# Output projection of the second half: all eight input tiles in one PSUM tile

## The chip, the cores and the metric

The kernel runs on one core of one Trainium2 chip. The metric is the device time of one execution in microseconds; the median of three executions is given. The engines are called as in the profile: PE (TensorE, matrix products), PEld (its weight loads), DVE (VectorE), ACT (ScalarE), POOL (GpSimd) and SP (SyncE, which issues most of the transfers). Each engine works through its own queue of instructions in order, and waits where an operand or a buffer isn't ready.

## The reference

One layer of a decoder, for 512 prompt tokens and 8 x 4 sample tokens (544 columns). A feed-forward block (FFN1), a mixing block and a second feed-forward block (FFN2), with a layer norm behind each:

```
x   = layer_norm(ALPHA * x + 0.5 * swiglu(x, ffn1), ln1)
proj = x @ w_in
y_rwkv = RWKV-7 recurrence over 8 heads of 64 (group norm, gate)   # 512 features
y_conv = c_b * conv3(c_c * c_h)                                    # 512 features
mix = concat(y_rwkv, y_conv) @ w_out                               # 1024 x 1024
x   = layer_norm(ALPHA * x + mix, ln2)
x   = layer_norm(ALPHA * x + 0.5 * swiglu(x, ffn2), ln3)
```

The change is in `mix` and in the sum that the second layer norm takes its mean from.

## The kernel before, in words

Features lie on the 128 partitions, tokens on the columns. So 1024 features are 8 tiles (`KD`), and the 544 columns are two halves, `HALF` = 0 to 256 and 256 to 544 (288 columns). Every product is done as three passes in a split format: weights and inputs are each split in a high part and a low part. `xhl` holds the input of the current product, split so. `mm3` (L146) issues for each input tile the matmuls high x high (L150), high x low (L151) and low x high (L152), and accumulates them in one PSUM tile. PSUM tiles named `mm` come from a pool of three (`big`), those named `sm` from a pool of five.

A weight tile is loaded by `wload` (L113): SP issues a 512 KB transfer into a tile `raw`; ACT writes the high part into a tile `hl` (`wsplit`, L134); DVE writes the low part (L135). A raw tile is free when both are done, an hl tile when its last matmul is done. Around the change there are two raw tiles and four hl tiles (three of the pool `wp` and one of `w4`). When FFN2 is opened (`f2.open`), three raw and three hl tiles are added, in memory that earlier stages have left, and the loads that use them may run ahead.

The 1024 input features of the output projection are eight tiles. Tiles 4 to 7 are the convolution part, tiles 0 and 1 the first two pairs of heads, tiles 2 and 3 the last two pairs, which the recurrence finishes last. The weights are packed to fit: `wo_c` has tiles 4 to 7 for two output tiles a load, `wo_0` tiles 0 and 1 for four output tiles, `wo_1` tiles 2 and 3 for four output tiles. `wout(h)` (L1402) does tiles 4 to 7, 0 and 1 of one half: 18 matmuls for each output tile `d`, and a DVE addition into `z` (L1420). `last(h)` (L1423) does tiles 2 and 3: 6 matmuls for each output tile, a second DVE addition into `z` (L1431), and an addition to the running sum over output tiles (`add_sum`, L320 and L322), from which the layer norm takes the mean.

The order of work is made by generators. `bg` is a queue of work that fills gaps; `take` runs its first generator for a given amount, and `weave` runs a generator on the critical chain (`gnorm`, `layer_norm`) and takes fill between its steps. A scheduler then sets the place of every instruction on its engine. Behind the recurrence come `last(0)` and the group norm of the last heads; then the layer norm of the first half, `l2a`, with `wout(1)` as fill; then the pools of the mixing block are closed, FFN2's are opened, `last(1)` runs by itself, and the layer norm of the second half, `l2b`, runs with `f2.first()` as fill (the gate and up products of FFN2's first four row tiles, for the first half). In `layer_norm` the sum (L222 for `l2b`, L227 and L228 for `l2a`) gives the mean, L235 subtracts it, L236 squares, L241 or L243 add the squares, L248 or again L222 sum them, L255 and L258 make the factor, L262 and L268 apply it, and L138 and L139 split the result into `xhl`.

Of the kernel before, what the change touches and what calls it, by code (L numbers as in the profile page):

```python
# [15 lines left out]
OP = mybir.AluOpType  # L16
# [13 lines left out]
HALF = ((0, 256), (256, 544))  # L30
# [31 lines left out]
def body(ctx: ExitStack, tc: tile.TileContext, xT, gu1, wd1, win, wo_c, wo_0, wo_1, gu2, wd2, lora, vec, cst,  # L62
         sst, cstate, s0, y_o, wkvp_o, wkvs_o, shift_o, conv_o):
    nc = tc.nc
    PE, ACT, DVE, POOL = nc.tensor, nc.scalar, nc.vector, nc.gpsimd
# [13 lines left out]
    xhl = keep.tile([P, 2, KD, T], F32R, name="xhl")  # L79
# [10 lines left out]
    def big():  # L90
        return ps.tile([P, 512], F32, name="mm", bufs=3)

    def sm():
        return ps.tile([P, 512], F32, name="sm", bufs=5)
# [15 lines left out]
    def wtiles():  # L110
        return raw_tile(), hl_tile()

    def wload(src, n=1024, parts=1):  # L113
        raw, hl = wtiles()
        m = n // parts
        for i in range(parts):
            dma(raw[:, i * m:i * m + m], src[:, i * m:i * m + m])
            wsplit(hl, raw, i * m, i * m + m)
        return hl

    def issue(prev, f, *args, **kw):
        with tc.issue_after(prev.ins):
            return f(*args, **kw)

    def after(ins, prev):
        info = mybir.DependencyInfo(mybir.DependencyClass.NoSync, mybir.DependencyReason.DATA)
        tc.add_manual_dep(ins.ins, prev.ins.name, info, reason="table order")
# [5 lines left out]
    def wsplit(hl, raw, a, b):  # L133
        ACT.activation(hl[:, 0, a:b], raw[:, a:b], AF.Copy)  # L134
        DVE.tensor_tensor(hl[:, 1, a:b], raw[:, a:b], hl[:, 0, a:b].bitcast(F32), op=OP.subtract)  # L135

    def split(hi, lo, x):
        ACT.activation(hi, x, AF.Copy)  # L138
        DVE.tensor_tensor(lo, x, hi.bitcast(F32), op=OP.subtract)  # L139

    def block(hl, j, i):
        if isinstance(hl, tuple):
            hl, i = hl[i // 4], i % 4
        return hl[:, j, i * P:(i + 1) * P]

    def mm3(out, hl, src, ks, c0, c1, off=0, start=True, stop=True):  # L146
        n = len(ks)
        for i, k in enumerate(ks):
            wh, wl = (block(hl, j, off + i) for j in range(2))
            PE.matmul(out, wh, src[:, 0, k, c0:c1], start=(start and i == 0), stop=False)  # L150
            PE.matmul(out, wh, src[:, 1, k, c0:c1], start=False, stop=False)  # L151
            seen["fill"] = PE.matmul(out, wl, src[:, 0, k, c0:c1], start=False, stop=(stop and i == n - 1))  # L152
            if i % 2 and not (stop and i == n - 1):
                yield 6 * ((c1 - c0) / 2.4 + 3)

    bg = deque()
# [22 lines left out]
    def take(need):  # L179
        while need > 0 and bg:  # L180
            g = bg[0]
            try:
                need -= next(g)
            except StopIteration:
                bg.popleft()

    def until(done):
        while not done():
            take(1)
# [10 lines left out]
    def weave(key, crit, *fill):  # L200
        bg.extend(fill)
        for need in crit:
            take(need * FILL[key])

    def drain(*fill):
        bg.extend(fill)
        take(1e9)
# [5 lines left out]
    def layer_norm(z, c0, c1, gcol, bcol, epsv, q, rs, s1, sink, table=None, hl2=None, both=False):  # L213
        n = c1 - c0
        pair = hl2 is None

        def mean_of(x, need):
            split(hl2[:, 0, :n], hl2[:, 1, :n], x)
            o = sm()
            yield need  # L220
            for i in range(2):
                PE.matmul(o[:, :n], onr, hl2[:, i, :n], start=(i == 0), stop=(i == 1))  # L222
            return o

        if pair:
            m = sm()
            PE.matmul(m[:, :n], ones, s1[:, :n], start=True, stop=False)  # L227
            PE.matmul(m[:, :n], ones, z[:, KD - 1, c0:c1], start=False, stop=True)  # L228
        else:
            m = yield from mean_of(s1[:, :n], 1300)  # L230
        yield 800 if pair else 300
        for j in range(4):
            zz = z[:, 2 * j:2 * j + 2, c0:c1]
            qq = q[:, 2 * j:2 * j + 2, :n]
            DVE.tensor_tensor(zz, zz, m[:, None, :n].to_broadcast([P, 2, n]), op=OP.subtract)  # L235
            sq = ACT.activation(qq, zz, AF.Square)  # L236
            if j == 0 and table == "ahead":
                tab = issue(sq, ACT.preload_act_table_set, "natural_log_exp_and_others")
            if pair:
                if j % 2:  # L240
                    DVE.tensor_tensor(q[:, 2 * j - 2:2 * j, :n], q[:, 2 * j - 2:2 * j, :n], qq, op=OP.add)  # L241
            elif j:
                DVE.tensor_tensor(q[:, 0:2, :n], q[:, 0:2, :n], qq, op=OP.add)  # L243
            yield 900 if pair else 1000
        if pair:
            v = sm()
            for i, j in enumerate((0, 1, 4, 5)):
                PE.matmul(v[:, :n], ones, q[:, j, :n], start=(i == 0), stop=(i == 3))  # L248
        else:
            DVE.tensor_tensor(q[:, 0, :n], q[:, 0, :n], q[:, 1, :n], op=OP.add)  # L250
            v = yield from mean_of(q[:, 0, :n], 900)
        yield 800 if pair else 600
        if table == "late":
            tab = issue(ACT.activation(warm, v[:, 0:1], AF.Copy), ACT.preload_act_table_set, "natural_log_exp_and_others")
        ln = ACT.activation(rs[:, :n], v[:, :n], AF.Ln, bias=epsv)  # L255
        if table:
            after(ln, tab)
        ACT.activation(rs[:, :n], rs[:, :n], AF.Exp, scale=-0.5)  # L258
        yield 1200 if pair else 600
        for d in range(0, KD, 2):  # L260
            zz = z[:, d:d + 2, c0:c1]
            DVE.tensor_tensor(zz, zz, rs[:, None, :n].to_broadcast([P, 2, n]), op=OP.mult)  # L262
            for e in (d, d + 1):
                x, g, b = z[:, e, c0:c1], col(gcol, e), col(bcol, e)
                if both and e > d:
                    DVE.tensor_scalar(x, x, g, b, op0=OP.mult, op1=OP.add)
                else:
                    ACT.activation(x, x, AF.Identity, scale=g, bias=b)  # L268
            sink(d, zz, c0, c1)
            yield 1600 if pair else 1700  # L270
# [36 lines left out]
    def to_x(spill):  # L307
        def sink(d, x, c0, c1):
            split(xhl[:, 0, d:d + 2, c0:c1], xhl[:, 1, d:d + 2, c0:c1], x)
            if spill:  # L310
                dma(xsp[:, d:d + 2, c0:c1], x)
        return sink
# [393 lines left out]
    z = pool(zst, "zp").tile([P, KD, T], F32, name="z")  # L706
# [657 lines left out]
    z = pool(ctx, "zp2", "right").tile([P, KD, T], F32, name="z")  # L1364
    yst = ExitStack()
    yp = pool(yst, "ys", "right")
    f2 = Ffn(z, gu2, wd2, "2", 4, 0)
# [34 lines left out]
    def wout(h):  # L1402
        c0, c1 = HALF[h]
        if h == 0:
            ys = [(k, yload(k)) for k in (0, 1)]
            for k in range(KD):
                ACT.activation(z[:, k], z[:, k], AF.Copy, scale=ALPHA)
            for k, y in ys:
                ysplit(k, y, 0, T)
        n = c1 - c0  # L1410
        for d in range(KD):
            if d % 4 == 0:
                w0 = wload(wo_0[d // 4])
            if d % 2 == 0:
                wc = wload(wo_c[d // 2])
            o = big()
            yield from mm3(o[:, :n], wc, xhl, (4, 5, 6, 7), c0, c1, (d % 2) * 4, stop=False)
            yield from mm3(o[:, :n], w0, xhl, (0, 1), c0, c1, (d % 4) * 2, start=False)
            zz = z[:, d, c0:c1]
            DVE.tensor_tensor(zz, zz, o[:, :n], op=OP.add)  # L1420
            yield 6 * 120

    def last(h):  # L1423
        c0, c1 = HALF[h]
        for d in range(KD):
            if d % 4 == 0:
                w = wload(wo_1[d // 4])
            o = big()
            yield from mm3(o[:, :c1 - c0], w, xhl, (2, 3), c0, c1, (d % 4) * 2)
            zz = z[:, d, c0:c1]  # L1430
            DVE.tensor_tensor(zz, zz, o[:, :c1 - c0], op=OP.add)  # L1431
            add_sum(f2.s1[h], z, d, c0, c1, KD if h else KD - 1)
            yield 6 * 120

    fin = []
# [20 lines left out]
    bg.appendleft(last_fin())  # L1456
    weave("g1", gnorm(1, 1, cp))
    until(lambda: len(fin) == 3)
    weave("l2a", layer_norm(z, *HALF[0], V_LN2G, V_LN2B, epsl, lnq, lnr, f2.s1[0], to_x(False)))
    drain()  # L1460
    wstate["ex_hl"] = []
# [5 lines left out]
    f2.s1[0] = s1  # L1467
    f2.open()
    lnq = f2.open_lnq()
    drain(last(1))  # L1470
    ln2b = layer_norm(z, *HALF[1], V_LN2G, V_LN2B, epsl, lnq, f2.lnr, f2.s1[1], to_x(False), "late", f2.hl2, True)
    weave("l2b", ln2b, f2.first())
    drain(f2.main())
# [85 lines left out]
```

## Time and profile before

| | us |
|---|---|
| median of three runs | 1093.47 (1092.75 to 1095.14) |
| the profiled execution | 1092.91 |
| its span, first to last instruction | 1091.1 |
| PE busy | 1059.4 (97%) |
| DVE busy | 845.7 (78%) |
| ACT busy | 588.3 (54%) |

Times in the views are counted from the span's start. The stretch around the change is 676 to 770 us: `last(0)` up to 684, `l2a` up to 705, `last(1)` up to 708, `l2b` up to 736, then FFN2. A row of a view by time has the start, the duration, the engine, the line and the operation with output and input; a bracket gives how long the engine had been idle and what ended the wait. The end of a matmul is modelled, and matmuls overlap: the distance between two starts, not the duration, is what a matmul costs PE.

### The profile page before, as it was taken

To read this page: it belongs to the slowest core of one execution; us is meant where nothing else is said; L and a number is where in the kernel's file an instruction comes from. 1 tells how busy PE (TensorE), PEld (TensorE's weight loads), DVE (VectorE), ACT (ScalarE), POOL (GpSimd) and SP (SyncE) were. 2 spreads that over 40 slices of the span, in tenths; PEclk is the share of its full clock that TensorE was granted. 3 is DMA by queue.
4 is the path that set the end of the run, shared out by engine and by line. 5 is a ranking of instruction groups with operands and counts; after the bars stand their busy time and mean duration, and the time that the engine had idled before them with its cause. 6 is when DMAs were issued, how large, how long until landed. Compare 5 with 4: busy or idle time off the path is not lost.

```text
span 1091.1 us, 22869 instructions
## 1 busy us (share of the span) xinstructions
PE 1059.4 (97%) x9258; PEld 1019.9 (93%) x9258; DVE 845.7 (78%) x1576; ACT 588.3 (54%) x1095; POOL 178.4 (16%) x288
## 2 busy tenths in 40 slices
PE   9999999999999998999999999999999999999997
PEld 8999999999999987898889987999999999999996
DVE  7788988889775857775578558999889888887657
ACT  6645465554552767653435334667555555545425
POOL 0122220313100022142000200001312213121000
PEclk9999999999999999999999999999999999999999
DMA  8568594967853323252145625443857859677402
GB/s 281 135 128 190 119 221 122 184 151 154 193 135 117 97 95 88 63 117 70 41 140 183 145 79 174 120 135 79 180 153 154 196 117 212 153 159 172 122 1 82
DMA packets 99082, 148.88 MB, mean 136 GB/s; under 512 B 35233, under 2 KB 60577, under 8 KB 98977
## 3 DMA queue, kind: packets, MB, share of 16 engines
q1 hardware_dynamic: 71776, 111.25, 33.2%
q0 software_dynamic: 27200, 36.18, 22.0%
q8 instruction: 72, 1.18, 0.4%
q14 instruction: 34, 0.27, 0.1%
HBM read 128.74 MB, written 9.75 MB: 127 GB/s over the span
## 4 chain that ended last, share of the span: by engine, by line
PE 68%; DVE 9%; issue 9%; ACT 7%; DMA 6%; POOL 1%; SPq 0%; POOLq 0%; DVEq 0%; ACTq 0%
PE mm L547 7%; PE mm L150 7%; PE mm L548 7%; PE mm L549 7%; PE mm L151 7%; PE mm L152 7%; PE sm L549 5%; PE sm L548 5%; PE sm L547 5%; DMA raw<-in_gu 4%; ACT hl L134 3%; DVE hl L135 2%; PE sm L1042 1%; PE sm L150 1%; PE sm L151 1%
## 5 line engine op out<-in xcount | busy, mean ns | idle before, releaser
L135 DVE TENSOR_TENSOR hl<-raw,hl 128x1024 fp32r<-128x1024 f32 (+3 forms) x232 | 270.5, 1171 | 75.2 <-ACT hl L134 74.2
L134 ACT ACTIVATE hl<-raw 128x1024 fp32r<-128x1024 f32 (+3 forms) x232 | 231.8, 1013 | 88.8 <-DVE raw L514 40.5
L150 PE MATMUL mm<-xhl,hl 128*128 128x288 f32 (+1 forms) x736 | 219.7, 299 | 3.2 <-DVE z L1431 1.6
L151 PE MATMUL mm<-xhl,hl 128*128 128x288 f32 (+1 forms) x736 | 214.1, 291 | 0.3 <-DVE xhl L139 0.3
L152 PE MATMUL mm<-xhl,hl 128*128 128x288 f32 (+1 forms) x736 | 212.6, 289 | 0.1
L150 PEld LDWEIGHTS mm<-xhl,hl 128*128 128x128 f32 x736 | 139.1, 189 | 10.3 <-DVE z L1431 2.6
L151 PEld LDWEIGHTS mm<-xhl,hl 128*128 128x128 f32 x736 | 139.4, 189 | 2.6 <-issue 1.2
L152 PEld LDWEIGHTS mm<-xhl,hl 128*128 128x128 f32 x736 | 139.2, 189 | 1.2 <-DVE hl L135 0.5
L549 PE MATMUL sm<-xhl,hl 128*128 128x272 f32 x432 | 125.3, 290 | 0.0
L548 PE MATMUL sm<-xhl,hl 128*128 128x272 f32 x432 | 124.5, 288 | 0.0
L547 PE MATMUL sm<-xhl,hl 128*128 128x272 f32 x432 | 124.0, 287 | 0.0
L547 PE MATMUL mm<-tv,hl 128*128 128x272 f32 x288 | 83.2, 289 | 3.4 <-ACT cpb L608 3.1
L520 POOL DMA_DIRECT2D raw<-in_gu x36 | 43.4, 1206 | 256.9 <-DVE hlb L139 155.3
L549 PE MATMUL mm<-tv,hl 128*128 128x272 f32 x288 | 83.4, 290 | 0.0
L548 PE MATMUL mm<-tv,hl 128*128 128x272 f32 x288 | 83.1, 289 | 0.0
L547 PEld LDWEIGHTS sm<-xhl,hl 128*128 128x128 f32 x432 | 81.4, 188 | 0.0
L549 PEld LDWEIGHTS sm<-xhl,hl 128*128 128x128 f32 x432 | 81.3, 188 | 0.0
L548 PEld LDWEIGHTS sm<-xhl,hl 128*128 128x128 f32 x432 | 81.2, 188 | 0.0
L526 POOL DMA_DIRECT2D raw<-in_wd x32 | 39.3, 1482 | 248.8 <-DVE hlb L139 218.0
L547 PEld LDWEIGHTS mm<-tv,hl 128*128 128x128 f32 x288 | 54.3, 188 | 4.7 <-ACT cpb L608 4.7
L547 PE MATMUL mm<-hhl,hl 128*128 128x272 f32 x192 | 56.9, 302 | 0.7 <-DVE z L637 0.7
L547 PE MATMUL sm<-hhl,hl 128*128 128x272 f32 x192 | 55.9, 291 | 0.0
(393 smaller groups left out, 2784.0 us busy)
## 6 DMA issues: line engine op xcount, KB each, us to landing
raw<-in_gu SPq DMA_DIRECT2D x84, 512.0 KB, 4.7
raw<-in_gu POOLq DMA_DIRECT2D x36, 512.0 KB, 6.3
raw<-in_wd SPq DMA_DIRECT2D x32, 512.0 KB, 4.7
raw<-in_win SPq DMA_DIRECT2D x26, 512.0 KB, 3.6
raw<-in_wd POOLq DMA_DIRECT2D x32, 256.0 KB, 6.9
raw<-in_wd SPq DMA_DIRECT2D x16, 384.0 KB, 3.2
z<-cpb POOLq DMA_DIRECT2D x16, 272.0 KB, 9.7
z<-sv POOLq DMA_DIRECT2D x16, 272.0 KB, 6.5
```

The source lines that it names most:

```text
L134: ACT.activation(hl[:, 0, a:b], raw[:, a:b], AF.Copy)
L135: DVE.tensor_tensor(hl[:, 1, a:b], raw[:, a:b], hl[:, 0, a:b].bitcast(F32), op=OP.subtract)
L150: PE.matmul(out, wh, src[:, 0, k, c0:c1], start=(start and i == 0), stop=False)
L151: PE.matmul(out, wh, src[:, 1, k, c0:c1], start=False, stop=False)
L152: seen["fill"] = PE.matmul(out, wl, src[:, 0, k, c0:c1], start=False, stop=(stop and i == n - 1))
L520: POOL.dma_start(x.rearrange("p (s c) -> p s c", s=2), bass.AP(tensor=a11.tensor, offset=a11.offset, ap=[[2 * D, P], [P * 2 * D, 2], [1, 5 ...
L526: POOL.dma_start(four(x)[:, i], bass.AP(tensor=a11.tensor, offset=a11.offset, ap=[[DFF, P], [P * DFF, 2], [1, 256]]), accum_op=OP.add)
L547: PE.matmul(out, wh, src(0, i), start=(first and i == 0), stop=False, skip_group_check=True)
L548: PE.matmul(out, wh, src(1, i), start=False, stop=False, skip_group_check=True)
L549: PE.matmul(out, wl, src(0, i), start=False, stop=(i == n - 1), skip_group_check=True)
L1042: crit(PE.matmul(q[r0:r0 + m, o:o + nn], lhs, rhs, start=True, stop=True))
```

## The change

`wout(1)` now looks whether the outputs of the last heads are there (the mark 4 in `fin`, set when the group norm and `last(0)` are done). For an output tile that is reached after that, all eight input tiles go into one PSUM tile: 24 matmuls, one DVE addition into `z`, and the addition to the sum. For an output tile reached earlier it does as before and puts the tile's number on a list, `left`; a new generator `rest()` does input tiles 2 and 3 of these, and `last(1)` is gone. `rest()` stands in `bg` behind `wout(1)`, so both are fill of `l2a`.

```
         n = c1 - c0
+        w1 = None
         for d in range(KD):
...
+            whole = h == 1 and 4 in fin
+            yield from mm3(o[:, :n], w0, xhl, (0, 1), c0, c1, (d % 4) * 2, start=False, stop=not whole)
             zz = z[:, d, c0:c1]
+            if whole:
+                if w1 is None or d % 4 == 0:
+                    w1 = wload(wo_1[d // 4])
+                yield from mm3(o[:, :n], w1, xhl, (2, 3), c0, c1, (d % 4) * 2, start=False)
+            elif h:
+                left.append(d)
             DVE.tensor_tensor(zz, zz, o[:, :n], op=OP.add)
+            if whole:
+                sums.append(d)
+                add_to(sums, f2.s1[1], z, d, c0, c1)
             yield 6 * 120
+    left, sums = [], []
+    def rest():
+        c0, c1 = HALF[1]
+        w = None
+        for d in left:
+            if w is None or d % 4 == 0:
+                w = wload(wo_1[d // 4])
+            o = big()
+            yield from mm3(o[:, :c1 - c0], w, xhl, (2, 3), c0, c1, (d % 4) * 2)
+            zz = z[:, d, c0:c1]
+            DVE.tensor_tensor(zz, zz, o[:, :c1 - c0], op=OP.add)
+            sums.append(d)
+            add_to(sums, f2.s1[1], z, d, c0, c1)
...
     until(lambda: len(fin) == 3)
+    fin.append(4)
+    bg.append(rest())
     weave("l2a", layer_norm(z, *HALF[0], V_LN2G, V_LN2B, epsl, lnq, lnr, f2.s1[0], to_x(False)))
...
-    drain(last(1))
```

`add_to` is the sum's addition for tiles that come in any order. Two of the eight output tiles, 0 and 1, are reached early and are left for `rest()`; six are whole.

In the rows that follow, a number behind a name tells one buffer from another. The transfers on SP, from the group norm of the last heads on, before:

```order
L117 DMA raw_8518<-in_wo_0 128x1024
L117 DMA raw_8523<-in_wo_c 128x1024
L117 DMA raw_8660<-in_wo_1 128x1024
L117 DMA raw_8700<-in_wo_1 128x1024
L117 DMA raw_8813<-in_gu2 128x1024
L117 DMA raw_8578<-in_wo_c 128x1024
L117 DMA raw_8744<-in_gu2 128x1024
L117 DMA raw_8749<-in_gu2 128x1024
L117 DMA raw_8818<-in_gu2 128x1024
```

The same place in the changed kernel:

```order
L117 DMA raw_8492<-in_wo_1 128x1024
L117 DMA raw_8539<-in_wo_0 128x1024
L117 DMA raw_8742<-in_gu2 128x1024
L117 DMA raw_8806<-in_gu2 128x1024
L117 DMA raw_8811<-in_gu2 128x1024
L117 DMA raw_8544<-in_wo_c 128x1024
L117 DMA raw_8573<-in_wo_1 128x1024
L117 DMA raw_8620<-in_wo_c 128x1024
L117 DMA raw_8694<-in_wo_1 128x1024
L117 DMA raw_8737<-in_gu2 128x1024
L117 DMA raw_8878<-in_gu2 128x1024
```

Before, the three early transfers into FFN2's added raw tiles (8660, 8700, 8813) bring both loads of `wo_1` and one of FFN2. Now they bring three of FFN2 (8742, 8806, 8811), and the loads of `wo_1`, three in place of two, go through the two old raw tiles, one after the other with `wo_0` and `wo_c`: 8492, 8544, 8620 and 8737 in one of them, 8539, 8573 and 8694 in the other.

PE, where output tile 3 ends and output tile 4 begins in `l2a`, before (`mm_8493` is tile 3, `mm_8528` and `mm_8551` are tiles 4 and 5; `lnq` are the squares of `l2a`):

```order
L152 MATMUL mm_8493<-xhl_68,hl_8244 128x288
L248 MATMUL sm_8558<-lnq_7140,ones_67 128x256
L150 MATMUL mm_8528<-xhl_68,hl_8524 128x288
L151 MATMUL mm_8528<-xhl_68,hl_8524 128x288
L150 MATMUL mm_8551<-xhl_68,hl_8524 128x288
L151 MATMUL mm_8551<-xhl_68,hl_8524 128x288
L248 MATMUL sm_8558<-lnq_7140,ones_67 128x256
L152 MATMUL mm_8528<-xhl_68,hl_8524 128x288
```

and in the changed kernel (`mm_8507` is tile 3, `mm_8549` and `mm_8588` are tiles 4 and 5; `hl_8493` holds `wo_1`):

```order
L152 MATMUL mm_8507<-xhl_68,hl_8493 128x288
L248 MATMUL sm_8562<-lnq_7140,ones_67 128x256 x2
L150 MATMUL mm_8549<-xhl_68,hl_8545 128x288
L151 MATMUL mm_8549<-xhl_68,hl_8545 128x288
L150 MATMUL mm_8588<-xhl_68,hl_8545 128x288
L151 MATMUL mm_8588<-xhl_68,hl_8545 128x288
L248 MATMUL sm_8562<-lnq_7140,ones_67 128x256 x2
L152 MATMUL mm_8549<-xhl_68,hl_8545 128x288
```

Tiles 4 and 5 now begin on `hl_8545`, whose raw tile is filled one load later than that of `hl_8524` was.

ACT, from the last split of `l2a` to the split of the sum for `l2b` (`hhl<-cpb`), before:

```order
L134 ACTIVATE hl_8745<-raw_8744 128x1024
L138 ACTIVATE xhl_68<-z_7136 128x2x256
L134 ACTIVATE hl_8750<-raw_8749 128x1024
L134 ACTIVATE hl_8814<-raw_8813 128x1024
L134 ACTIVATE hl_8819<-raw_8818 128x1024
L134 ACTIVATE hl_8886<-raw_8885 128x1024
L134 ACTIVATE hl_8891<-raw_8890 128x1024
L399 ACT_TABLE_LOAD
L399 ACTIVATE hk_8654<-mm_8754 128x256
L138 ACTIVATE hhl_8653<-cpb_71 128x288
```

and in the changed kernel:

```order
L138 ACTIVATE xhl_68<-z_7136 128x2x256
L134 ACTIVATE hl_8738<-raw_8737 128x1024
L134 ACTIVATE hl_8743<-raw_8742 128x1024
L134 ACTIVATE hl_8695<-raw_8694 128x1024
L134 ACTIVATE hl_8807<-raw_8806 128x1024
L134 ACTIVATE hl_8812<-raw_8811 128x1024
L134 ACTIVATE hl_8879<-raw_8878 128x1024
L134 ACTIVATE hlb_8952<-raw_8951 128x512
L134 ACTIVATE hlb_8953<-raw_8951 128x512
L399 ACT_TABLE_LOAD
L399 ACTIVATE hk_8728<-mm_8747 128x256
L138 ACTIVATE hhl_8727<-cpb_71 128x288
```

`hl_8695` (`wo_1` for `rest()`) stands behind `hl_8738`, FFN2's first weight, and two half splits more stand ahead of the split of the sum.

More of the change, by code (lines that the diff above doesn't have):

```diff
@@ L1417, in wout, with add_to @@
             yield from mm3(o[:, :n], wc, xhl, (4, 5, 6, 7), c0, c1, (d % 2) * 4, stop=False)
-            yield from mm3(o[:, :n], w0, xhl, (0, 1), c0, c1, (d % 4) * 2, start=False)
+            whole = h == 1 and 4 in fin
+            yield from mm3(o[:, :n], w0, xhl, (0, 1), c0, c1, (d % 4) * 2, start=False, stop=not whole)
             zz = z[:, d, c0:c1]
-            DVE.tensor_tensor(zz, zz, o[:, :n], op=OP.add)
+            if whole:
[4 more added lines that the diff above has]
+                left.append(d)
+            DVE.tensor_tensor(zz, zz, o[:, :n], op=OP.add)
+            if whole:
+                sums.append(d)
+                add_to(sums, f2.s1[1], z, d, c0, c1)
+            yield 6 * 120
+    left, sums = [], []
+    def add_to(seen_, s1_, z_, d, c0, c1):
+        s = s1_[:, :c1 - c0]
+        if len(seen_) == 2:
+            DVE.tensor_tensor(s, z_[:, seen_[0], c0:c1], z_[:, d, c0:c1], op=OP.add)
+        elif len(seen_) > 2:
+            DVE.tensor_tensor(s, s, z_[:, d, c0:c1], op=OP.add)
+    def rest():
[10 more added lines that the diff above has]
+            add_to(sums, f2.s1[1], z, d, c0, c1)
             yield 6 * 120
```

## The prediction

> **What bounds the kernel now.** I read four views: the page's first part, the waits of PE around the change, the stretches of 8 us there, and the timelines of PE, DVE, ACT and SP.
>
> ```profile
> PE 1059.4 (97%) x9258; PEld 1019.9 (93%) x9258; DVE 845.7 (78%) x1576; ACT 588.3 (54%) x1095; POOL 178.4 (16%) x288
> 684.00:692.00 8.00, 7.91 (x52) 7.01 (x51) 7.77 (x12) 5.07 (x7) 0.00 (x0) 1.00 0.28 80
> 700.00:708.00 8.00, 7.29 (x56) 7.06 (x55) 7.97 (x18) 7.05 (x10) 0.00 (x0) 1.00 0.44 133
> 716.00:724.00 8.00, 7.09 (x61) 6.89 (x60) 6.70 (x11) 3.86 (x8) 0.00 (x0) 1.00 0.57 192
> PE mm L150 <- DVE z L1431: 1.6, 2, 0.9
> PE sm L222 <- ACT hhl L138: 0.9, 1, 0.9
> PE mm L547 <- DVE z L637: 0.7, 1, 0.7
> ```
>
> The stretches give the busy time of PE, PEld, DVE, ACT and POOL in that order. PE is the bound, and the change removes no matmul from it, so only its waits can move. The three rows of waits are all that PE has from 676 to 770 us, 3.2 us. DVE is almost as full (7.97 of 8). Two of these waits lie in the reach of the change:
>
> ```profile
> 705.38 0.40 PE L150 MATMUL mm<-xhl,hl 128*128 128x288 f32 x1 [0.71 <-DVE z L1431]
> 712.89 0.29 PE L222 MATMUL sm<-hhl,ones 128*128 128x288 f32 x1
> 723.69 0.40 PE L222 MATMUL sm<-hhl,ones 128*128 128x288 f32 x1 [0.91 <-ACT hhl L138]
> ```
>
> The first is `last(1)` waiting for a PSUM tile; the last is the second sum of `l2b`. The other wait on L1431 is that of `last(0)`, ahead of the change, and that on L637 lies behind it; both stay.
>
> **The change part by part.** *What goes.* Six DVE additions of a 288-column tile are not needed, and with 24 matmuls per tile in place of 6 the wait of 0.71 us goes. At 723.69 the chain of `l2b` (subtract, square, add, split) was late, since two half splits that waited for loads stood among its squares on ACT. In the new order all splits stand ahead of the squares; from the first L222 pair, at 717 by (e), I count a DVE split and 6.9 us of the chain to 725.2, and PE's 74 matmuls of `f2.first` end at 725.8. So I let the 0.91 us go too. Together 1.6 us off. One weight load more costs DVE and ACT a split each:
>
> ```profile
> L135 DVE TENSOR_TENSOR hl<-raw,hl 128x1024 fp32r<-128x1024 f32 x10 | 12.0, 1219 | 0.1
> L134 ACT ACTIVATE hl<-raw 128x1024 fp32r<-128x1024 f32 x11 | 11.1, 1046 | 2.3 <-DMA raw<-in_gu 1.5 <-PE mm L152 0.8
> L134 ACT ACTIVATE hlb<-raw 128x512 fp32r<-128x512 f32 x2 | 1.2, 624 | 2.3 <-DMA raw<-in_gu 2.3
> L262 DVE TENSOR_TENSOR z<-z,lnr 128x512 f32<-128x512 f32 x4 | 2.6, 686 | 1.4 <-ACT lnr L258 1.4
> L1420 DVE TENSOR_TENSOR z<-z,mm 128x288 f32<-128x288 f32 x7 | 3.1, 449 | 0.1
> ```
>
> Six additions are 6 x 0.45 = 2.7 us, the split 1.2 us: DVE is 1.5 us lighter, ACT 1.0 us heavier. The PE passes of `last(1)` move under `l2a` unchanged.
>
> *What is new: weights in two raw tiles.* Before, both loads of `wo_1` had raw tiles of their own, filled early. Now seven loads pass through two raw tiles. Each costs a transfer, an ACT split (1.05) and a DVE split (1.2) before the next may be issued. The prices:
>
> ```profile
> DMA to landing us min/median/max: 3.5/4.2/6.3
> 685.52 0.33 SPq L117 DMA_DIRECT2D raw<-in_wo_c  x1
> 690.56 13.79 SPq L117 DMA_DIRECT2D raw<-in_gu  x5
> raw<-in_gu SPq DMA_DIRECT2D x1, 512.0 KB, 3.6
> raw<-in_gu SPq DMA_DIRECT2D x1, 512.0 KB, 5.8
> 703.16 3.89 ACT L134 ACTIVATE hl<-raw 128x1024 fp32r<-128x1024 f32 x4
> 688.16 1.06 ACT L134 ACTIVATE hl<-raw 128x1024 fp32r<-128x1024 f32 x1 [0.85 <-PE mm L152]
> 689.32 1.22 DVE L135 TENSOR_TENSOR hl<-raw,hl 128x1024 fp32r<-128x1024 f32 x1
> 685.17 0.29 PE L150 MATMUL mm<-xhl,hl 128*128 128x288 f32 x1
> 688.62 0.29 PE L152 MATMUL mm<-xhl,hl 128*128 128x288 f32 x1
> 688.75 0.59 PE L248 MATMUL sm<-lnq,ones 128*128 128x256 f32 x2
> 689.27 0.40 PE L150 MATMUL mm<-xhl,hl 128*128 128x288 f32 x1
> ```
>
> The first row is of the loads from 655 to 715 us; the load issued at 690.56 landed in 3.6 us, one issued at 693.6 with another under way in 5.8. Four ACT splits in a row take 3.89 us, a step of 0.95. From 685.17 to 688.62 are 26 steps: 0.133 us a matmul (256 columns: 0.117 by the rows below). An L248 is 0.52. The ACT row shows a split that waits for its hl tile, which the last matmul of `wo_c` for tiles 2 and 3 frees; DVE follows 0.1 us behind ACT, and SP issues 0.02 us behind DVE (690.56). Now I follow the new order with these prices.
>
> *(a) Tile 4.* Tile 2 has six matmuls more, so the hl tile is free 0.8 us later, at 688.96. ACT splits `wo_0` (to 690.0), squares (to 690.5), splits `wo_c` (to 691.5). PE reaches L248 at 688.75 + 12 x 0.133 = 690.3, does two (to 691.4) and waits 0.2 us for the high half. The next pair of L248 needs the second L241, which DVE reaches behind the split of `wo_0` (691.3) and the addition of tile 3, at 692.3: a wait of 0.3. The low half needs one more DVE split, to 693.8, against PE's 693.4: 0.4. Sum 0.9 us; bounds 0.5 (ACT and DVE each a little earlier) and 1.2.
>
> *(b) `wo_1` for tiles 4 to 7.* Its raw tile is free at 691.3, the load lands 3.6 us later if it is alone, at 695.0; ACT to 696.0. PE comes at 693.9 + 16 x 0.133 = 696.0. High and low half together 0.2 us; bounds 0 and, for a landing in 5.8, 2.0.
>
> *(c) `wo_c` for tiles 6 and 7.* Raw tile free at 693.8, median landing 698.0, ACT to 699.1, DVE to 700.4 behind L262 and L139 (0.6 us a step); PE needs the low half at 700.3. 0.2 us; bounds 0 and 1.4.
>
> *(d) FFN2's first weight and `rest()`.* The raw tile is free at 700.4, the load lands at 704.65, and ACT's queue has `hl_8738`, `hl_8743`, `hl_8695`: 704.7 + 0.95 + 0.95 + 1.05 = 707.65. PE wants `hl_8695` at 700.5 + 45 x 0.133 = 706.45 and waits 1.2 us. Behind it `mm_8747` needs the PSUM tile of `mm_8662`, whose addition stands on DVE behind the splits of 8738 and 8743 (708.5, PE there at 708.2): 0.3. Sum 1.5 us. A landing of 3.5 makes it 0.7, one of 5.6 makes it 2.7.
>
> *(e) The split of the sum for `l2b`.* Rows of ACT before:
>
> ```profile
> 708.55 1.06 ACT L134 ACTIVATE hl<-raw 128x1024 fp32r<-128x1024 f32 x1 [1.50 <-DMA raw<-in_gu]
> 709.63 1.28 ACT L399 ACT_TABLE_LOAD   x1
> 711.20 0.44 ACT L138 ACTIVATE hhl<-cpb 128x288 fp32r<-128x288 f32 x1
> 680.91 0.28 PE L151 MATMUL mm<-xhl,hl 128*128 128x256 f32 x1
> 681.03 0.28 PE L152 MATMUL mm<-xhl,hl 128*128 128x256 f32 x1
> ```
>
> Before, the split came at 711.20 and PE used it at 712.89 without a wait. Now `hl_8879`'s load is issued when DVE has split 8738 (707.0), lands at 711.4 and is split by 712.45; the half splits wait for a raw tile that is free at 708.1 and lands in some 5 us (713.3), to 714.4; the table load and the Silu make it 716.0, the split 716.4. PE is at L222 at 710.8 + 36 x 0.117 = 715.0. A wait of 1.4 us; bounds 0.5 and 2.0. What hides nothing here is PE: L222 stands in its queue ahead of the other fill.
>
> *Elsewhere.* One load more shifts the ring of raw and hl tiles through all of FFN2, and some loads swap places on SP. FFN1 and FFN2 run the same code from different places of the ring, and their waits in the main part show what that is worth:
>
> ```profile
> PE mm L547 <- ACT cpb L608: 1.1, 2, 0.6
> PE mm L547 <- ACT cpb L608: 2.0, 2, 1.7
> ```
>
> The first is 100 to 320 us, the second 780 to 1000 us: a difference of 0.9 us, so 0 with bounds of 0.9 each way.
>
> *Sum.* New waits 0.9 + 0.2 + 0.2 + 1.5 + 1.4 = 4.2 us, old ones 1.6 us: +2.6 us. The profiled execution has 1092.91 us (span 1091.1) and lies 0.56 us below the median of 1093.47. I predict 1095.5 for the profile's own time and 1096.1 for the median. With the low ends together, 0.5 + 0 + 0 + 0.7 + 0.5 - 1.6, it is +0.1; with b, d and e at their high ends and c caught up by b, +5.6.
>
> [...]
>
> **The rivals.** *1, not slower: the loads keep up.* If 8573, 8620 and 8737 all land in about 3.5 us, the shortest of the row, (a) is 0.6, (b) and (c) 0, (d) 0.7 and (e) 0.5, since ACT and DVE then reach the split of the sum sooner: 1.8 - 1.6 = +0.2 us, 1093.7. It decides where a load lands before 695.0, 698.2 and 703.5. For it: the raw tiles are free early enough for a quick load. Against it: the median is 4.2, since loads of several tiles are under way together.
>
> *2, slower: each load lands late*, near 5.7 us. (a) 0.9, (b) 2.0, (c) 0, (d) 2.7, (e) 1.6: 7.2 - 1.6 = +5.6 us, 1099.1. For it: 6.3 us at most was measured. Against it: these loads follow each other, two at a time at most.
>
> *3: the waits bring the clock down.* In this trace it happens:
>
> ```profile
> PE sm L881 <- ACT kq L878: 4.0, 2, 3.4
> 390.00:400.00 10.00, 8.23 (x49) 7.87 (x48) 6.30 (x12) 5.95 (x14) 1.97 (x5) 0.83 0.54 172
> 680.68 0.39 PE L150 MATMUL mm<-xhl,hl 128*128 128x256 f32 x1 [0.85 <-DVE z L1431]
> 676.00:684.00 8.00, 7.00 (x53) 6.26 (x51) 7.77 (x22) 2.23 (x4) 0.00 (x0) 1.00 0.73 262
> ```
>
> The third figure from the end of a stretch is the granted clock. A wait of 3.4 us, and 0.83 in those 10 us: 10 x 0.17 = 1.7 us more, 1097.8. My longest wait is 1.4 us, and with the wait of 0.85 us at 680.68 the clock stayed at 1.00. [...]
>
> *4, faster: DVE is the true bound* from 676 to 716, where it is 7.77 to 7.97 of 8 busy, and its 1.5 us less come on top of the 1.6 us: -2.7 to -3.1 us, about 1090.6. Against it: PE, not DVE, is what everything else waits for; PE waited on DVE 0.7 us there.
>
> That the change doesn't do what it says is no rival: six whole tiles stand in the order, two are left.
>
> **How the numbers follow.** What can be told from no change is 0.2%, 2.2 us. The forecast (+2.6, its own range +0.8 to +4.5, 1094.3 to 1098.0) has 0.50; about seven tenths of it lie over +2.2. Rival 1 has 0.29, rival 2 0.11, rival 3 0.04, rival 4 0.06. Slower by over 0.2%: 0.36 + 0.11 + 0.04, about 0.52. Within 0.2%: 0.14 + 0.28, 0.42. Faster: 0.06. The range for 8 in 10 takes in rivals 1 and 2 with the ring's 0.9: 1092.6 to 1099.4.
>
> **What would show it.** Right: PE waits on hl splits (L134, L135) at output tile 4, on L134 at `rest()`, and on ACT's L138 at the first L222 of `l2b`; no wait of `mm` on an addition in 700 to 708, none at the second L222; SP waiting on L135 between the loads of `wo_1` and `wo_c`. Wrong: none of these waits, or a new wait behind 760 us in FFN2, which I have put at 0.

## The result

The changed kernel took 1097.22 us (median of 9 runs, 1093.47 to 1105.93) against 1094.52 us before (9 runs, 1090.84 to 1096.76): a ratio of 1.0045, 95% interval 1.0023 to 1.0066. Two more comparisons, made for the experiments, gave 1.0019 (0.9999 to 1.0038) and 1.0031 (1.0014 to 1.0048). The mean of the three is 1.0032, 3.5 us more. The two medians are 2.7 us apart, but the ratio stands for 4.9 us. The forecast was 2.6 us more, slower likelier than not: the direction held, the size was too small by the ratios, and 1097.22 lies inside the range.

The profiled execution has 1096.39 us and a span of 1094.6 us, 3.5 us more than before. The same part of the program in both, from the first L227 of `l2a` to FFN2's first L547, as one stretch (its length behind the colon pair, then the busy time of PE, PEld, DVE, ACT and POOL with the instructions that touch the stretch; the third figure from the end is the granted clock). Before:

```profile
684.10:757.88 73.78, 72.06 (x549) 70.27 (x549) 66.94 (x113) 53.12 (x89) 4.92 (x4) 1.00 0.46 122
```

and after:

```profile
684.63:760.56 75.93, 73.05 (x550) 70.54 (x549) 66.08 (x107) 54.49 (x90) 4.92 (x4) 1.00 0.45 126
```

PE does the same matmuls (the 550th is the L547 that ends the stretch) and needs 2.15 us more, though DVE is 0.86 us lighter. PE's waits of the changed kernel in 676 to 775 us, by line waited for (total, times, longest):

```profile
PE sm L222 <- ACT hhl L138: 1.4, 1, 1.4
PE mm L150 <- DVE z L1465: 0.9, 1, 0.9
PE mm L150 <- ACT hl L134: 0.8, 2, 0.6
PE mm L547 <- DVE z L637: 0.8, 1, 0.8
PE mm L152 <- DVE hl L135: 0.4, 1, 0.4
PE mm L150 <- ACT xhl L138: 0.3, 1, 0.3
```

and where they stand in PE's timeline, with the last matmul ahead of the longest and the pair of the second sum:

```profile
692.04 0.40 PE L150 MATMUL mm<-xhl,hl 128*128 128x288 f32 x1 [0.17 <-ACT hl L134]
694.30 0.40 PE L152 MATMUL mm<-xhl,hl 128*128 128x288 f32 x1 [0.37 <-DVE hl L135]
707.65 0.40 PE L150 MATMUL mm<-xhl,hl 128*128 128x288 f32 x1 [0.60 <-ACT hl L134]
714.98 0.28 PE L150 MATMUL mm<-xhl,hl 128*128 128x256 f32 x1
716.62 0.40 PE L222 MATMUL sm<-hhl,ones 128*128 128x288 f32 x1 [1.37 <-ACT hhl L138]
726.62 0.40 PE L222 MATMUL sm<-hhl,ones 128*128 128x288 f32 x1
```

The old waits are gone: none on an addition behind 685 (L1465 is `last(0)`, L1431 before), and the second sum, which waited 0.91 us, has no bracket now. In their place are those that the prediction named: the weights of output tile 4 at 692.04 and 694.30, `rest()` at 707.65, the first sum of `l2b` at 716.62. The one of 0.3 us on L138 stands at the end of the layer norm, at 736.64, and the prediction had no term for it. What holds the first sum up is ACT's row ahead of its split of the sum:

```profile
704.64 4.85 ACT L134 ACTIVATE hl<-raw 128x1024 fp32r<-128x1024 f32 x5 [0.97 <-DMA raw<-in_gu]
711.52 1.06 ACT L134 ACTIVATE hl<-raw 128x1024 fp32r<-128x1024 f32 x1 [2.02 <-DMA raw<-in_gu]
713.39 1.16 ACT L134 ACTIVATE hlb<-raw 128x512 fp32r<-128x512 f32 x2 [0.81 <-DMA raw<-in_gu]
714.56 1.28 ACT L399 ACT_TABLE_LOAD   x1
715.86 0.38 ACT L399 ACTIVATE hk<-mm 128x256 f32<-128x256 f32 x1
716.14 0.43 ACT L138 ACTIVATE hhl<-cpb 128x288 fp32r<-128x288 f32 x1
```

ACT idles three times for weights of FFN2, the last time at the two half splits that now stand ahead of the split of the sum. A second place differs in this pair of traces. In FFN2's main part, behind 775 us, PE waited 2.0 us on L608 before; now it is

```profile
PE mm L547 <- ACT cpb L614: 3.0, 1, 3.0
PE mm L547 <- ACT cpb L608: 0.2, 1, 0.2
```

1.2 us more, at 996 us. I had put this part at 0, so it came first.

### The profile page after: what moved, and what is told of

The parts are those of the page before. It is cut to its first block, busy times and chain, and to the rows that moved or that the text cites. A ratio compares the mean times of both kernels' runs of the same rounds, so it can differ in the third digit from the quotient of the medians.

```text
span 1094.6 us, 22855 instructions
## 1 busy us (share of the span) xinstructions
PE 1061.4 (97%) x9258; PEld 1020.5 (93%) x9258; DVE 845.3 (77%) x1571; ACT 590.7 (54%) x1096; POOL 178.2 (16%) x288
## 4 chain that ended last, share of the span: by engine, by line
PE 68%; DVE 10%; issue 7%; ACT 7%; DMA 6%; POOL 1%; SPq 0%; DVEq 0%; POOLq 0%; ACTq 0%
PE mm L547 8%; PE mm L548 8%; PE mm L549 8%; PE mm L150 6%; PE mm L151 6%; PE mm L152 6%; PE sm L549 6%; PE sm L547 5%; PE sm L548 5%; ACT hl L134 2%; DVE hl L135 2%; DMA z<-sv 2%; DMA raw<-in_gu 2%; PE sm L1042 1%; PE sm L150 1%
## 5 line engine op out<-in xcount | busy, mean ns | idle before, releaser
L135 DVE TENSOR_TENSOR hl<-raw,hl 128x1024 fp32r<-128x1024 f32 (+3 forms) x233 | 272.1, 1171 | 76.9 <-ACT hl L134 75.6
L134 ACT ACTIVATE hl<-raw 128x1024 fp32r<-128x1024 f32 (+3 forms) x233 | 233.6, 1013 | 81.1 <-DVE raw L514 33.0
L547 PE MATMUL sm<-xhl,hl 128*128 128x272 f32 x432 | 124.0, 287 | 0.0
L547 PE MATMUL mm<-tv,hl 128*128 128x272 f32 x288 | 83.2, 289 | 4.2 <-ACT cpb L614 3.0
L547 PEld LDWEIGHTS sm<-xhl,hl 128*128 128x128 f32 x432 | 81.4, 188 | 0.0
L547 PEld LDWEIGHTS mm<-tv,hl 128*128 128x128 f32 x288 | 54.3, 188 | 5.5 <-ACT cpb L614 3.5
L547 PE MATMUL mm<-hhl,hl 128*128 128x272 f32 x192 | 56.9, 302 | 0.8 <-DVE z L637 0.8
L547 PE MATMUL sm<-hhl,hl 128*128 128x272 f32 x192 | 55.9, 291 | 0.0
```

Of the source, the lines that this page charges most:

```text
L547: PE.matmul(out, wh, src(0, i), start=(first and i == 0), stop=False, skip_group_check=True)
```

## The experiments

**Is it FFN2's load order?** The change turns the raw ring by one tile, and SP then issues some loads of FFN2 in another order. Two kernels change that and nothing else; PE, DVE, ACT and POOL keep their rows. Before, with the ring of the changed kernel:

```
-            self.raw, self.held, self.t = {}, [], 0
+            self.raw, self.held, self.t = {}, [], 0; wstate["raw"] += 1 * (self.ph == "2"); wstate["hl"] += 0 * (self.ph == "2")
```

> The kernel before, with nothing of the change but the raw ring of FFN2's main part turned on by one tile, as the change turns it: PE, DVE, ACT and POOL have the same instructions in the same order, only SP issues some FFN2 loads in another order. Theory A (the slowdown is made by the new waits of the output projection, the ring is worth 0): the time of before, 1.000 within 0.002; in FFN2, PE waits 2.0 us on L608 as in the trace of before and not on L614. Theory B (a good part of the slowdown is the new load order in FFN2, which lets the accumulating transfer of the last down-projection land late): slower by 1.2 us or more (1.001 to 1.003), and PE waits about 3 us on ACT's L614 behind L572, which stands on the transfer into z. Theory C (that wait comes from the time at which PE arrives there, some 2 us later than before, and not from SP's order): no wait on L614 here.

And the changed kernel, turned back (four further on a ring of five is one back):

```
-            self.raw, self.held, self.t = {}, [], 0
+            self.raw, self.held, self.t = {}, [], 0; wstate["raw"] += 4 * (self.ph == "2"); wstate["hl"] += 0 * (self.ph == "2")
```

> The changed kernel with the raw ring of FFN2's main part turned back by one tile: all engines as in the changed kernel, only SP has the load order of before in FFN2. Theory A: the slowdown of the changed kernel stays, 1.003 to 1.006, and the waits of 676 to 775 us are those of the changed kernel (about 3.5 us with the old one of 0.9 us on L1465). Theory B: it gets back 1.2 us or more, ratio 1.001 to 1.003, and the wait of 3 us on L614 is gone, with some 2 us on L608 in its place. Theory C: the wait of 3 us on L614 stays.

Measured: e1_before_ring 1.0009 (0.9992 to 1.0027), e2_after_ringback 1.0060 (1.0039 to 1.0081). PE's waits in FFN2's main part, first of e1_before_ring:

```profile
PE mm L547 <- ACT cpb L614: 0.6, 1, 0.6
PE mm L547 <- ACT cpb L608: 0.3, 1, 0.3
```

then of e2_after_ringback:

```profile
PE mm L547 <- ACT cpb L608: 0.6, 2, 0.4
PE mm L547 <- ACT cpb L614: 0.2, 1, 0.2
```

Theory B falls by its waits: the new order does not bring the 3.0 us to the kernel before, and the old one does not make the changed kernel faster. (The interval of e1_before_ring alone does not exclude the 1.001 to 1.003 that theory B asked for.) The wait of 2.0 us on L608, which theory A expected in e1_before_ring, isn't there either. The waits on L608 and L614 differ from one execution to the next: in four more executions of the changed kernel they sum to 1.8, 1.4, 1.0 and 1.3 us. They hang on when POOL's accumulating transfer into `z` lands (POOL began to issue it at 980.4 us in both traces, and ACT, which waits for it, went on at 992.48 in the changed kernel's and at 988.70 in that of before), and the 3.0 us was one draw of that. Over the six executions with the changed kernel's rows (its five and e2_after_ringback) they have a mean of 1.6 us, over the two with the rows of before 1.5 us. Putting FFN2 at 0 was right. In e2_after_ringback the stretch from L227 to L547 is 76.41 us, and in e1_before_ring, a second look at the kernel before, 74.07 us, its second sum waiting 1.2 us: the slowdown sits there. Why the ratio of e2_after_ringback is above those of the changed kernel stays open; its profiled execution, 1094.39 us, was the fastest of twelve.

**Which part of the change makes it?** First the move alone: no whole tiles, all eight left to `rest()` under `l2a`.

```
-            whole = h == 1 and 4 in fin
+            whole = False
```

> The changed kernel without the tiles that take all eight inputs: every output tile of the second half is left to rest(), which runs as filling under l2a. It has two loads of wo_1 as before, so FFN2's load order is that of before. Theory A (each whole tile's loads and the split of the sum make the waits): no wait at output tile 4 and none of 1.4 us at the first sum of l2b's layer norm; 0.999 to 1.001. Theory B says nothing else here, since the ring is not shifted: no 3 us on L614. If moving the last heads' part from between l2a and l2b to under l2a is itself what costs (less is left between the two layer norms to cover the first half's end), it is slower by 1 to 3 us, 1.001 to 1.003, with waits on DVE or on L138 between 700 and 725 us.

1.0025 (1.0009 to 1.0041). The waits at tile 4 and at the first sum are gone, as theory A has it, but the kernel is not back at the time of before, as theory A also had it: the ratio is that of the third reading, that moving the part under `l2a` itself costs, though its wait on L138 came at 735 us and not before 725. In its trace the stretch is 79.18 us, with a wait of 0.94 us on L135 at 709.6 and one of 1.5 us on L138 at 735, and, new, two pieces at half clock. The pieces of 3.4 us around them:

```profile
706.50:709.90 3.40, 2.21 (x13) 1.59 (x13) 3.40 (x9) 1.74 (x2) 0.00 (x0) 1.00 0.00 0
709.90:713.30 3.40, 3.40 (x18) 3.40 (x18) 2.68 (x4) 0.45 (x1) 0.00 (x0) 0.50 0.62 188
733.80:737.20 3.40, 1.60 (x10) 1.36 (x11) 3.40 (x7) 3.39 (x7) 0.00 (x0) 1.00 0.00 0
737.20:740.60 3.40, 3.40 (x16) 3.40 (x16) 2.83 (x5) 1.48 (x3) 0.00 (x0) 0.50 0.00 0
```

So here 3.4 us in which PE began only 13 or 10 matmuls (where PE was busy throughout, it was 31 in after_p3 from 723.50 us and 32 in the first trace of the changed kernel from 718.80 us) were followed by 3.4 us at a clock of 0.50, by an estimate from these rows 1.7 us on top of the wait (3.4 x 0.50). The waits themselves are of 0.3 to 1.5 us. That speaks against the prediction's rival 3, which went by a wait of 3.4 us. How far the third reading holds is answered by the last experiment below.

Then the whole tiles, with `rest()` put where `last(1)` was:

```
     fin.append(4)
-    bg.append(rest())
...
     lnq = f2.open_lnq()
+    drain(rest())
```

> The changed kernel with the whole tiles, but rest() run where last(1) ran before, after FFN2's tiles are opened. FFN2's ring is shifted as in the changed kernel. Theory A: the waits at output tile 4 (0.5 us) stay, the wait of 0.6 us at rest() and the one of 1.4 us at the first sum change, since rest()'s load now has FFN2's tiles; 1.001 to 1.005. Theory B: 3 us on L614 as in the changed kernel. If the early opening is what crowds the loads, it is faster than the changed kernel by 1 us or more.

1.0021 (0.9997 to 1.0046), which does not part it from the changed kernel. The stretch is 76.04 us with the same waits: 0.4 us on L135 at tile 4, 0.5 us on L134 at `rest()`, 1.7 us at the first sum. So nothing here shows that the place of `rest()` costs; its load of `wo_1` and the order on ACT are the same.

**The first sum.** Here PE's two matmuls of the first sum are put 13 matmuls of `f2.first` further back, so that they have work ahead of them while ACT is late:

```
-            m = yield from mean_of(s1[:, :n], 1300)
+            m = yield from mean_of(s1[:, :n], 1300 + 3000 * (table == "late"), table == "late")
...
-            for i in range(2):
-                PE.matmul(o[:, :n], onr, hl2[:, i, :n], start=(i == 0), stop=(i == 1))
+            with tc.issue_after(seen["fill"].ins) if behind else ExitStack():
+                [PE.matmul(o[:, :n], onr, hl2[:, i, :n], start=(i == 0), stop=(i == 1)) for i in range(2)]
```

> The changed kernel with PE's first sum of l2b's layer norm put 13 matmuls of f2.first further back, so that PE has work while ACT splits the sum (the wait of 1.37 us at that place in the changed kernel's trace, 1.8 us in another execution of the same stretch). Theory D1 (that wait is the largest single part of the slowdown, and by itself or with the waits near it also brings the clock down in some executions): the wait at L222 is gone or under 0.3 us, and the ratio is 1.000 to 1.003. Theory D2 (the wait is paid anyway, since the filling that covers it now is missing at the end of the layer norm): another wait of 1 to 2 us, on L138 or L139, stands between 725 and 745 us, and the ratio stays at 1.004 to 1.006.

1.0013 (0.9990 to 1.0037). L222 stands without a wait, and about half of what that saves comes back at the end of the layer norm, where the filling is short:

```profile
718.15 0.89 PE L222 MATMUL sm<-hhl,ones 128*128 128x288 f32 x2
735.65 0.54 PE L150 MATMUL mm<-xhl,hlb 128*128 128x288 f32 x2 [0.89 <-ACT xhl L138]
736.50 0.40 PE L151 MATMUL mm<-xhl,hlb 128*128 128x288 f32 x1 [0.31 <-DVE xhl L139]
```

Between D1 and D2, then: the ratio is D1's, part of the wait went where D2 put it, and no piece at half clock lies between 684 and 1088 us (the span is 1093.0 us). The stretch took 75.67 us, hardly less than the 75.93 us of the changed kernel's first trace and the 76.41 us of e2_after_ringback, which have no half clock there either. What the lower ratio comes from, one trace doesn't show.

**The changed kernel again.** Four more executions of it were profiled, since one trace can't show what happens in some executions only.

> The changed kernel once more, to see another execution of it. From the first L227 near 684 us to the first L547 near 760 us the changed kernel took 75.9 us, and a kernel with the same stretch 76.4, against 73.8 before: 2.2 to 2.6 us more. Theory A' (the stretch is all): here too 75.5 to 76.5 us, and no more stretches of half clock than before. Theory D (part of the slowdown is the clock: a stretch of 3.4 us at half clock behind a window in which PE had too little work): in an execution whose mean clock is 0.993 or less, such a stretch lies behind 684 us, near 710 to 720 or 980 to 1000 us, where the kernel before had none.

after_p2 and after_p3, one execution each, had the same expectation, and after_again this one:

> The changed kernel on the same chip as the run before, for a ratio of its own: 1.002 to 1.005 by both theories, with a wait of 1.2 to 2.3 us at the first L222; a half clock near 720 us only where that wait is near 2 us.

The ratios are those given above (1.0019 for after_p1, 1.0031 for after_again). The first L222 in after_p1, after_p2, after_p3 and after_again:

```profile
718.21 0.40 PE L222 MATMUL sm<-hhl,ones 128*128 128x288 f32 x1 [1.17 <-ACT hhl L138]
```

```profile
719.59 0.40 PE L222 MATMUL sm<-hhl,ones 128*128 128x288 f32 x1 [2.07 <-ACT hhl L138]
```

```profile
719.17 0.40 PE L222 MATMUL sm<-hhl,ones 128*128 128x288 f32 x1 [2.35 <-ACT hhl L138]
```

```profile
720.57 0.40 PE L222 MATMUL sm<-hhl,ones 128*128 128x288 f32 x1 [1.80 <-ACT hhl L138]
```

and the pieces of 3.4 us around it in after_p3:

```profile
716.70:720.10 3.40, 1.05 (x9) 0.93 (x8) 1.31 (x3) 3.37 (x6) 0.00 (x0) 1.00 0.91 305
720.10:723.50 3.40, 3.40 (x18) 3.40 (x17) 3.40 (x6) 1.69 (x3) 0.00 (x0) 0.50 0.35 77
723.50:726.90 3.40, 3.40 (x31) 3.40 (x30) 2.14 (x4) 2.10 (x4) 0.00 (x0) 1.00 0.30 114
```

The stretch from L227 to L547 took 75.72, 78.05, 78.34 and 77.85 us. In the last three a piece at half clock stands between 720 and 725 us; in after_p1, in the first trace (1.37 us) and in e2_after_ringback (1.79 us) none. Theory D holds: in three of six executions the wait at the first sum is followed by 3.4 us at half clock. The wait's own size comes from the half splits: ACT idled 0.81 us for their load in the first trace, 0.56, 1.46 and 1.09 us in after_p1, after_p2 and after_again, 1.29 us in e2_after_ringback, and here, in after_p3,

```profile
715.94 1.15 ACT L134 ACTIVATE hlb<-raw 128x512 fp32r<-128x512 f32 x2 [1.77 <-DMA raw<-in_gu]
```

In each of the six, PE's wait is 0.5 to 0.7 us longer than that. The six stretches have a mean of 77.05 us against 73.78 before (74.07 in e1_before_ring): 3.3 us more (3.1 by the mean of those two), close to the 3.5 us of the three ratios.

**Without the third load.** If the extra load of `wo_1` is behind this, the two early tiles can take their inputs 2 and 3 right behind tile 3, from the weights that are loaded there anyway:

```
             yield 6 * 120
+            yield from rest(w1) if whole and d == 3 else ()
...
-    def rest():
+    def rest(w=None):
         c0, c1 = HALF[1]
-        w = None
-        for d in left:
-            if w is None or d % 4 == 0:
+        while left:
+            d = left.pop(0)
+            if w is None:
```

> The changed kernel with the two tiles that are left over done right behind output tile 3, with the high and low halves of wo_1 that are loaded there for tiles 2 and 3, so that wo_1 is loaded twice as before and not three times, and the ring is not shifted. If the extra load is what makes the waits at rest() (0.6 us), at output tile 4 (0.5 us: PE now has 12 matmuls more ahead of it) and the late split of the sum (1.2 to 2.3 us), with the clock drop behind it: the stretch from L227 to L547 takes 72.5 to 74.5 us (73.8 before, 75.7 to 78.3 in the changed kernel), the wait at the first L222 is under 0.8 us, no half clock near 720 us, and the ratio is 0.998 to 1.001. If it is the whole tiles as such (seven loads between f2's weights on two raw tiles), the stretch stays at 75 us or more, and the ratio at 1.002 to 1.005.

1.0017 (1.0004 to 1.0030). Half of it came as expected: the wait at the first sum is gone, and so is the half clock near 720. On ACT the split of that sum now stands at 710.84, ahead of the half splits at 717.82. The wait for a low half at tile 4 stayed (L135, 0.6 us), so the third load is not behind it, and where `rest()` waited PE now waits for FFN2's first weight (L134). PE's waits in the stretch are now

```profile
PE mm L150 <- ACT xhl L138: 1.2, 1, 1.2
PE mm L150 <- ACT hl L134: 0.8, 1, 0.8
PE mm L151 <- DVE xhl L139: 0.6, 1, 0.6
PE mm L152 <- DVE hl L135: 0.6, 1, 0.6
```

with a piece at half clock from 735.2, and a length of 76.90 us. The first comes from ACT (the last experiment below tests this), where the order written for the new program put a Silu (L399) between the steps of the layer norm's root, so that the table is changed back and forth:

```profile
722.86 1.28 ACT L123 ACT_TABLE_LOAD   x1
724.15 1.28 ACT L399 ACT_TABLE_LOAD   x1
725.44 0.38 ACT L399 ACTIVATE sv<-mm 128x256 f32<-128x256 f32 x1
725.84 1.28 ACT L255 ACT_TABLE_LOAD   x1
727.14 0.50 ACT L255 ACTIVATE cpb<-sm,eps 128x288 f32<-128x288 f32 x1
727.66 1.28 ACT L258 ACT_TABLE_LOAD   x1
```

e3_under has the same three extra loads of 1.28 us, at 726.32, 728.01 and 729.83, and so its wait at 735. With that Silu held ahead of the first of them:

```
-            tab = issue(ACT.activation(warm, v[:, 0:1], AF.Copy), ACT.preload_act_table_set, "natural_log_exp_and_others")
+            tab = issue(issue(seen["silu"], ACT.activation, warm, v[:, 0:1], AF.Copy), ACT.preload_act_table_set, "natural_log_exp_and_others")
...
-            ACT.activation(s, g[:, :n], AF.Silu)
+            seen["silu"] = ACT.activation(s, g[:, :n], AF.Silu)
```

> The kernel with the two tiles done behind output tile 3, and with ACT's Silu of FFN2's third row put ahead of the table load for the logarithm, where the run before had it between logarithm and exponential at the price of three more table loads of 1.28 us each. There the wait at L222 had gone, but waits of 1.2 us (L138) and 0.6 us (L139) and a half clock stood at 731 to 738 us. If these came from the three table loads: both waits go or stay under 0.5 us in sum, no half clock behind 684 us, the stretch from L227 to L547 takes 73.3 to 74.5 us (73.8 before), and the ratio is 0.999 to 1.001. If moving the last heads' part under l2a leaves too little filling for l2b in any order: waits of 1 us or more between 725 and 745 us remain, the stretch is 75 us or more, and the ratio 1.0015 to 1.003.

0.9989 (0.9966 to 1.0012): the time of before. The stretch, and PE's waits in it:

```profile
685.37:759.29 73.92, 71.87 (x550) 70.56 (x549) 64.83 (x106) 54.37 (x89) 4.92 (x4) 1.00 0.45 122
```

```profile
PE mm L150 <- ACT hl L134: 1.2, 1, 1.2
PE mm L152 <- DVE hl L135: 0.6, 1, 0.6
PE mm L151 <- DVE xhl L139: 0.3, 1, 0.3
```

No half clock lies behind 684 us until the program's end. So neither the whole tiles nor the move under `l2a` cost anything that these runs can tell, and they win nothing: 2.1 us of waits, most of it for FFN2's first weight and for tile 4's low half, have taken the place of the old 1.6 us on the addition and on the second sum. The wait at the first sum stands in the kernels that load `wo_1` three times (the changed one, e2_after_ringback, e4_restlate) and in none that load it twice (e3_under, e6_inplace, e7_tables). The edit that takes the third load out also moves two tiles, and the runs do not part these two; for e6_inplace and e7_tables there is one trace each. None of these kernels is faster than the one before.

## Why the prediction was right in direction and too small

Two steps failed. Term (e), the wait at the first sum, was mis-sized: 1.4 us in the sum, 1.8 us measured on the mean. And the sum had nothing for the clock, because rival 3 went by a wait of 3.4 us: half clock came behind waits of 1.8 to 2.35 us and cost, by the estimate below, 0.85 us on the mean. Term (d) was mis-sized the other way, 1.5 us against 0.6.

*What goes*: right. Both waits, 0.71 and 0.91 us, are gone in all six executions, and the six additions are off DVE. Rival 4 falls: DVE is 0.86 us lighter in the stretch and the stretch is longer.

*(a) Tile 4*, 0.9 us: the place is right and the waits smaller, 0.17 us for the high half and 0.37 us for the low half; the 0.3 us ahead of L248 isn't there.

*(b) and (c)*, 0.2 us each: no wait; both loads were in time.

*(d) `rest()`*, 1.5 us: 0.60 us. FFN2's first weight was split from 704.64 on, as worked out (704.7), but this execution was 0.5 us late there from before the change, and PE came at 707.05 and not at 706.45. The wait on the PSUM tile (0.3) did not come.

*(e) The first sum*: mis-sized. I had 1.4 us with bounds of 0.5 and 2.0; the six executions have 1.37, 1.17, 2.07, 2.35, 1.80 and 1.79 us, 1.8 us on the mean, and two lie above the bound. The chain was the right one (ring, load of the half splits, table load, Silu, split), and the first trace follows it almost to the tenth; but "lands in some 5 us" is a spread, not a number: ACT's idle time for that load alone was 0.56 to 1.77 us in the six executions. Everything behind it in ACT's queue, the table load, the Silu and the split, is late by as much.

*Rival 3, the clock*, chance 0.04: its reading of the trace failed, since its rows do not belong together. I joined the wait of 3.4 us at L881 with the 0.83 of 390 to 400 us. In the trace of before the half clock follows a wait of 1.5 us, and the long wait, some 30 us later, is followed by full clock:

```profile
391.63 0.53 PE L150 MATMUL mm<-xhl,hl 128*128 128x288 f32 x2 [1.51 <-ACT xhl L138]
393.60:397.00 3.40, 3.40 (x17) 3.40 (x16) 2.70 (x5) 1.92 (x3) 1.02 (x2) 0.50 0.65 176
426.23 1.24 PE L881 MATMUL sm<-kq,cs 128*128 128x256 f32 x4 [3.37 <-ACT kq L878]
427.70:431.10 3.40, 3.40 (x44) 3.24 (x44) 1.01 (x3) 1.37 (x2) 0.10 (x1) 1.00 0.51 154
```

So the trace of before does not tie the drop to a wait of 3.4 us: half clock stood behind one of 1.51 us, the size of (e). In the stretch it came in three of six executions behind a wait of 1.8 to 2.35 us. With 3.4 us at a clock of 0.50 each time, 1.7 us, an estimate of the cost is 0.85 us on the mean.

*The price of a wait.* The rows show 1.16 us more of idle time in the stretch of the first trace (75.93 - 73.05 against 73.78 - 72.06), and the stretch is 2.15 us longer with the same matmuls. The difference is in how a wait is counted: from 714.98 to 716.62 are 1.64 us where 0.12 are usual, 1.52 us lost, and the bracket says 1.37. This wait cost 0.15 us more than its bracket. The stretch has five waits in place of two; with 0.15 us for each, an estimate, that is about half of the 0.99 us, and where the rest goes was not traced.

*Sum.* Forecast +2.6 us, as (a) to (e) 4.2 less 1.6. The stretch shows +2.15 us in the first trace, and over the six 3.3 us: 2.4 us without the half clock (3 x 1.7 / 6 = 0.85). The terms that were too large, (a) to (d), 2.8 us against 1.1, hid that (e), the clock and the price of a wait were too small. That the first stretch and the two medians come near 2.6 us is in part luck: errors that cancel. A slip in the prediction's sum changes nothing here: with b, d and e at their high ends it is 6.0 us, not 5.6. Rival 1 (all loads in time) held for (b) and (c), rival 2 (each load late) for the half splits.

*Elsewhere*, 0 with bounds of 0.9: right on the mean. The first pair of traces spoke against it with 1.2 us, and the two ring experiments cleared it.

## What to carry to other kernels

Added filling has a second cost in the order that it leaves on the queues behind it (here one more load put two splits ahead of the one that PE needed, and in two variants an activation fell between table loads), so follow each queue to the next instruction that PE waits for, and price a load ahead of it by the spread of its landings, not by their median (ACT idled 0.56 to 1.77 us for the same load over six executions). A wait of PE of one to two us can have a clock drop beside it: here waits of 1.17 to 2.35 us at the first sum were followed by a clock of 0.50 in three of six executions. Before a condition is taken from a trace, the wait and the drop should be looked up in order of time. Take several traces before a place is blamed: a single pair showed 1.2 us in FFN2 that were not the change's.

## What the runs showed of the hardware

In these traces the granted clock fell to 0.50 behind waits far shorter than 3.4 us: behind 0.94 and 1.54 us in e3_under (from 709.9 and from 737.2 us on), 1.51 us in the trace of before (from 393.6 us), and 2.07, 2.35 and 1.80 us in after_p2, after_p3 and after_again (from 720.9, 720.1 and 721.2 us). Each of these pieces at half clock was 3.4 us long. The length of a wait did not decide it: 1.79 us in e2_after_ringback and 1.71 us in e4_restlate, at the first sum, had no half clock behind them, where 1.80 us in after_again had. The wait of 3.37 us at L881 ended at 426.23 us in the trace of before, with a clock of 1.00 behind it, and at 425.25 us in the first trace of the changed kernel, with a clock of 0.50 from 425.2 to 428.6 us. Nor did PE's work in the 3.4 us ahead decide it. With 9 to 14 matmuls, PE busy for 1.05 to 2.21 us, half clock followed (after_p2, after_p3, after_again, e3_under); with 14, PE busy for 1.78 us (e4_restlate, from 715.65 us), and with 8, busy for 1.50 us (before, from 424.31 us), it did not. So neither gives a limit here, and what decides was not shown.

A program's own spread is of this size too: ahead of 684 us the thirteen traces hold between 3.4 us (e3_under) and 13.7 us (after_again) at half clock, in kernels that are all but the same there, and the waits on L608 and L614 in FFN1, far ahead of the change and with the same instructions, summed to 1.1 us in the trace of before and to 2.0 us in that of e1_before_ring.
